# Output projection of a flow-matching backbone: 14 of 17 row tiles in pairs by seven products of quarters, with sums of the weights kept in DRAM

## The chip, the cores and the metric

The kernel runs on one core of one Trainium2 chip. The metric is device time in microseconds, from one launch to its end; of several executions the median counts. The profile comes from one further execution, whose own time is given beside its span.

## The reference, cut to what matters

One layer, no depth loop, two request groups: 128 context tokens and 2048 sample tokens, 2176 rows in all, 1024 channels. Input projection and three mixer branches stand ahead; what the change touches is the end:

```
gt = jax.nn.sigmoid(gates.reshape(B, T, N_BRANCH, D_MODEL))
merged = jnp.einsum('btnd,btnd->btd', gt, pb)
return jnp.einsum('btd,de->bte', merged, w_out), s_f, s_b
...
h = h + gate[:, None, :] * out
y_sample = rmsnorm(h, final_g)
```

So each of 17 tiles of 128 rows of `merged` is multiplied by the 1024 x 1024 matrix `w_out`, times a gate for each channel, plus the row of x, then a final RMSNorm. All is float32; the kernel splits each float32 operand into a high and a low half of float16 and makes three products (high by high, high by low, low by high) of each.

## The kernel before, in words

**Stages.** After the mixers come three merge passes (`merge`, lines 1672 to 1721), one for each branch. A pass runs over eight blocks of 128 channels; in each block it goes over two halves of the tokens, and for each group of up to 512 tokens it makes a gate product (24 matmuls, ScalarE takes the sigmoid from PSUM, L1699) and a branch product (12 matmuls, VectorE multiplies from PSUM, L1708); GpSimd adds the result to the row of partial sums, which is read from DRAM and written back there (`mD`, L1687, L1709, L1716). The rows live in the tag `mrow` of the pool `big`, two buffers.

**The last merge** (L1812) takes the upper half of the tokens first (tiles 8 to 16), then tiles 0 to 7. In each block it also loads one eighth of `w_out` and splits it (`out_w`, L1759, by `load_w`: a square for the scale on ScalarE, a scale by a one-column matmul and three small VectorE operations L264 to L266, a high half L311, a low half L312). In the last block, when the upper half is written, `ahead_out` (L1792) prepares the first five tiles in the order 16, 8, 9, 10, 11, while the last half's products still run. `out_prep` (L1765) loads a tile of the merged rows (SyncE, L1767), squares it (ScalarE, L1777), makes the scale, the high half (ScalarE, L1779), the low half (VectorE, L1780) and a row of eight scales (L1782).

**The output projection** (L1823 to 1863) takes the 17 tiles one by one. A tile is two halves of 512 columns, 24 matmuls each into one PSUM bank (`gemm_N`, L331): 48. VectorE multiplies each bank by the scaled gate (L1841), GpSimd adds the row of x (L1842); the gate itself is scaled for each tile by GpSimd (`scale_gate`, L1802). Then the row's square (ScalarE, L1860), a power on GpSimd (L251), the scaling of the row (VectorE, L1862) and the store. Tile i + 5 is prepared after tile i. The last tile has column groups of 512, 384 and 128 and its own end.

**What sets the order.** The kernel is written on a framework with pools of tiles. Each tag of a pool has a fixed number of buffers; a new tile takes a buffer in the order in which the text asks for it, and waits for the last reader of the tile before it. A pool that is opened where others were closed (`op`, L1816, after `big` and `bwp` are closed at L1813) takes their memory. The order of the instructions on each engine, and of the DMA issues on each queue, is fixed when the program is built: a planner takes, by its own estimate of the time, the instruction that is ready and comes first in the text; `tc.high_priority()` moves some forward. SyncE's loads and stores share one queue (SP), GpSimd's DMAs another.

The tag `wst` of the pool `wp`, two buffers of 128 x 1024, holds weights on their way in, and tiles of merged rows at the hand-over. `xh` and `xl` are the high and low halves of the normalised input, read by every gate product.

Of the kernel before, what the change touches and what calls it, by code (L numbers as in the profile page):

```python
# [20 lines left out]
P = 128  # L21
D = 1024
KT = 8
# [165 lines left out]
def hybrid_flow_kernel(ctx: ExitStack, tc: tile.TileContext, x_prompt, x_sample, state_delta, c, c_ctx, w_ada,  # L189
# [50 lines left out]
    def mm(out, l, r, start=True, stop=True):  # L240
        newest[0] = PE.matmul(out, l, r, start=start, stop=stop)  # L241
# [98 lines left out]
    def xrows(t0, n):  # L340
        return xs_[t0:t0 + n, :] if t0 < NS else xp_[t0 - NS:t0 - NS + n, :]
# [1415 lines left out]
    winv = sb(orp, [P, KT], "winv8")  # L1757

    def out_w(i):  # L1759
        w = load_w(w_outb[i], KT, hi=whi[:, :, i * P:(i + 1) * P], lo=wlo[:, :, i * P:(i + 1) * P])  # L1760
        V.tensor_mul(winv[:, i:i + 1], w.inv, sx)

    turn = []

    def out_prep(t, pl, tag, hl=None):  # L1765
        mt = sb(pl, [P, KT, P], tag, bufs=2)
        SY.dma_start(mt, mD[:, :, t * P:(t + 1) * P].rearrange("k p t -> p k t"))  # L1767
        if hl is None:
            mh = sb(orp, [P, KT, P], "mh", F16, bufs=3)
            ml = sb(orp, [P, KT, P], "ml", F16, bufs=3)  # L1770
        else:
            mh = sb(wp, [P, KT, P], "whi", F16, bufs=4)
            ml = sb(wp, [P, KT, P], "wlo", F16, bufs=4)
        ss = sb(orp, [P, 1], "mss", bufs=2)
        with tc.high_priority():
            with tc.issue_after(turn[0].ins) if len(turn) > 2 else ExitStack():
                A.activation(ml, mt, AF.Square, accum_out=ss)  # L1777
            s, inv = scales(ss, orp, "msc")
            turn.append(A.activation(mh, mt, AF.Copy, scale=s))  # L1779
            V.scalar_tensor_tensor(ml, mt, s, mh, ALU.mult, ALU.subtract)  # L1780
        inv8 = sb(orp, [P, KT], "inv8", bufs=6)
        V.tensor_scalar(inv8, winv, inv, None, ALU.mult)  # L1782
        return mh, ml, inv8

    pre, gp = [], []

    def half_gate(i):
        t = sb(ep, [P, 512], "st", bufs=3)
        SY.dma_start(t, gateD[1:2, i * 512:(i + 1) * 512].to_broadcast([P, 512]))
        gp.append(t)  # L1790

    def ahead_out(h0):  # L1792
        if h0:
            for i, t in enumerate(order[:5]):
                pre.append(out_prep(t, *((wp, "wst") if i % 3 else (big, "mrow")), None if i < 3 else wp))
            for i in range(2):
                half_gate(i)
                scale_gate(gp[i], gp[i], pre[0][2][:, 4 * i:4 * i + 4])
# [6 lines left out]
    order = [16] + list(range(8, 16)) + list(range(8))  # L1805
    def tail(db):
        out_w(db)
        if db == KT - 1:
            for _ in gates:
                pass  # L1810
# [5 lines left out]
    op = pool(ctx, "op", 2)  # L1816
    gb = sb(op, [P, D], "gb", bufs=1)
    SY.dma_start(gb, gateD[0:1, :].to_broadcast([P, D]))
    fg = sb(op, [P, D], "fg", bufs=1)
    SY.dma_start(fg, final_g[None, :].to_broadcast([P, D]))  # L1820

    part = sb(op, [P, 3], "part", bufs=1)
    for i_, t in enumerate(order):  # L1823
        mh, ml, inv8 = pre[i_]
        end = i_ == 16
        xr = sb(op, [P, D], "xr")
        SY.dma_start(xr, xrows(t * P, P))
        hh = sb(op, [P, D], "hh")
        ss2 = sb(op, [P, 1], "hss")
        if i_:  # L1830
            gt = sb(op, [P, D], "gt")
            scale_gate(gt, gb, inv8)
        if end:
            hf = sb(op, [P, D], "gt")
        for i, (c0, c1) in enumerate([(0, 512), (512, 896), (896, D)] if end else [(0, 512), (512, D)]):
# [3 lines left out]
            dst, gc = (hh[:, cs], gt[:, cs]) if i_ else (gp[i], gp[i])  # L1839
# [10 lines left out]
        if i_ < 12:  # L1850
            pre.append(out_prep(order[i_ + 5], op, "mt"))
# [40 lines left out]
```

## Time and profile before

| what | value |
|---|---|
| runs shown | 2181.92, 2181.95, 2177.65 us |
| median | 2181.92 us |
| profiled execution, its own time | 2174.15 us |
| its span, first to last instruction | 2172.3 us |
| granted TensorE clock, mean | 0.995 |
| TensorE busy | 2102.9 us of the span |
| VectorE, ScalarE, GpSimd busy | 1314.2, 1037.8, 704.2 us |
| HBM read and written | 241.48 and 127.62 MB |
| last merge and output projection | about 1724 us to the end |

How to read it: the page names engines PE (TensorE), PEld (its weight loads), DVE (VectorE), ACT (ScalarE), POOL (GpSimd), SP (SyncE); a small q behind a name is that engine's instruction queue. A row of a group gives line, engine, operation, output<-inputs, shapes and count, then busy time and mean ns of one, then the idle time of the engine ahead of them and what ended it. A row of a time line gives start and duration in us, and in brackets the idle time ahead. A row of the windows gives, for a stretch, the busy time of PE, PEld, DVE, ACT and POOL (with the number of instructions), the granted clock, the share of the DMA engines and the GB/s. Columns named `x` behind a count merge that many instructions. Products are matmuls of L241, whatever stage they belong to.

### The profile page before, as it was taken

The page shows a single profiled execution, that of the slowest core. Times are in us where ns is not written, and L with a number is a line of the kernel's source. Part 1 is how long each engine was busy: PE and PEld are TensorE (multiplying, and loading weights), DVE is VectorE, ACT ScalarE, POOL GpSimd, SP SyncE. Part 2 cuts the span into 40 slices and gives each one's busy share as a digit, 9 for nine tenths or more (in the row PEclk, how much of TensorE's full clock was granted, in tenths as well). Part 3 has the DMA queues.
Part 4 walks back from the last instruction along what each step waited for, and adds up shares of the span by engine and source line. Part 5 has one row for each costly group of instructions (what it writes and reads, how often), then busy time and mean ns, then how long its engine had stood idle before and what let it go on. Part 6 is the DMA issues. An engine that isn't in the chain of part 4 may idle for free. (4 is left out here: it accounts for less than half of the span.)

```text
span 2172.3 us, 42588 instructions
## 1 busy us (share of the span) xinstructions
PE 2102.9 (97%) x16249; PEld 1204.3 (55%) x16249; DVE 1314.2 (60%) x3049; ACT 1037.8 (48%) x2388; POOL 704.2 (32%) x869
## 2 busy tenths in 40 slices
PE   8999999999899999999899999899999999999998
PEld 4455444465455677787455556556555544444444
DVE  6657754389779798466655556765563544233454
ACT  5554744466556664455544446655553422222332
POOL 0321332233434422444222223354532222212543
PEclk9999999999999999999999999999999999999999
DMA  9525632276776743444755556776664533334542
GB/s 353 218 72 201 250 119 83 93 234 218 235 235 218 227 141 91 138 142 119 234 163 160 164 168 188 239 216 198 195 199 139 177 129 122 114 102 132 170 149 103
DMA packets 228748, 371.90 MB, mean 171 GB/s; under 512 B 38952, under 2 KB 125504, under 8 KB 226240
## 3 DMA queue, kind: packets, MB, share of 16 engines
q1 hardware_dynamic: 176032, 274.20, 40.3%
q0 software_dynamic: 12688, 51.27, 6.5%
q10 hardware_dynamic: 39824, 43.72, 6.0%
q8 instruction: 127, 2.08, 0.4%
q14 instruction: 77, 0.63, 0.1%
HBM read 241.48 MB, written 127.62 MB: 170 GB/s over the span
## 5 line engine op out<-in xcount | busy, mean ns | idle before, releaser
L241 PE MATMUL b<-xh,whi 128*128 128x512 f16 (+1 forms) x1920 | 649.7, 347 | 2.8 <-DVE sg L1436 2.5
L241 PE MATMUL b<-xl,whi 128*128 128x512 f16 (+1 forms) x1920 | 650.0, 347 | 0.0
L241 PE MATMUL b<-xh,wlo 128*128 128x512 f16 (+1 forms) x1920 | 649.0, 347 | 0.0
L241 PEld LDWEIGHTS <-whi 128*128 128x128 f16 x3904 | 355.7, 98 | 327.9 <-issue 8.6
L241 PEld LDWEIGHTS <-wlo 128*128 128x128 f16 x1952 | 191.0, 98 | 176.9 <-issue 1.4
L241 PE MATMUL b<-big,bhi 128*128 128x512 f16 (+1 forms) x960 | 250.8, 347 | 4.2 <-ACT big L1669 2.6
L1709 POOL TENSOR_TENSOR mrow<-mrow,sg 128x512 f32<-128x512 f32 (+1 forms) x80 | 93.4, 1169 | 283.2 <-DVE sg L1708 173.0
L241 PE MATMUL b<-big,blo 128*128 128x512 f16 (+1 forms) x480 | 162.9, 347 | 0.2 <-DVE blo L312 0.2
L1699 ACT ACTIVATE sg<-b,winv 128x512 f32<-128x512 f32 (+1 forms) x120 | 74.1, 618 | 132.6 <-PE b L241 132.1
L241 PEld LDWEIGHTS <-xh 128*128 128x128 f16 x1496 | 118.3, 99 | 30.0 <-issue 1.8
L1708 DVE SCALAR_TENSOR_TENSOR sg<-b,binv,sg 128x512 f32<-128x512 f32 (+1 forms) x80 | 53.4, 668 | 129.0 <-PE b L241 120.8
L241 PEld LDWEIGHTS <-bhi 128*128 128x128 f16 x960 | 86.4, 98 | 79.8 <-issue 4.4
L936 POOL TENSOR_TENSOR cy<-cy,raw 128x545 f32<-128x545 f32 (+1 forms) x48 | 64.4, 1366 | 180.6 <-ACT raw L935 180.6
L255 DVE CAST wscb<-wss 128x1 bf16<-128x1 f32 x89 | 13.7, 154 | 138.2 <-ACT wlo L299 57.6
L241 PE MATMUL b<-whi,xh 128*128 128x128 f16 x544 | 94.5, 221 | 1.8 <-DVE yT L1622 1.0
L1170 POOL COPY T<-ES 32x256 f16<-32x256 f16 x68 | 29.2, 430 | 201.2 <-DMA ES<-ei 178.2
L241 PE MATMUL b<-wlo,xh 128*128 128x128 f16 x544 | 94.4, 221 | 0.0
L241 PE MATMUL b<-whi,xl 128*128 128x128 f16 x544 | 94.4, 221 | 0.0
L241 PE MATMUL b<-wohi,mh 128*128 128x512 f16 (+2 forms) x248 | 91.9, 372 | 0.2 <-ACT mh L1779 0.2
L241 PE MATMUL b<-wohi,ml 128*128 128x512 f16 (+2 forms) x248 | 91.7, 372 | 0.3 <-DVE ml L1780 0.3
L241 PE MATMUL b<-wolo,mh 128*128 128x512 f16 (+2 forms) x248 | 91.9, 372 | 0.0
L312 DVE SCALAR_TENSOR_TENSOR wlo<-wst,wsc,whi 128x1024 f16<-128x1024 f32 x52 | 71.2, 1370 | 33.1 <-ACT whi L311 32.9
(481 smaller groups left out, 4241.3 us busy)
## 6 DMA issues: line engine op xcount, KB each, us to landing
wst<-in_w_blk_dram SPq DMA_DIRECT2D x58, 512.0 KB, 5.7
qkv<-cy POOLq DMA_DIRECT2D x12, 1089.0 KB, 5.3
st<-br SPq DMA_DIRECT2D x48, 256.0 KB, 3.8
mrow<-mrg SPq DMA_DIRECT2D x18, 512.0 KB, 3.8
mrow<-mrg SPq DMA_DIRECT2D x16, 576.0 KB, 4.4
mrg<-mrow POOLq DMA_DIRECT2D x16, 576.0 KB, 3.9
dc<-dec SPq DMA_DIRECT2D x17, 512.0 KB, 4.4
kq<-qkv SPq DMA_DIRECT2D x34, 256.0 KB, 4.9
```

What stands on the lines that cost most here:

```text
L241: newest[0] = PE.matmul(out, l, r, start=start, stop=stop)
L255: V.tensor_copy(sb16, ss)
L312: w.low = V.scalar_tensor_tensor(w.lo, st, s, w.hi, ALU.mult, ALU.subtract)
L936: G.tensor_tensor(y[:, c0:c1], y[:, c0:c1], raw[:, 1 + c0:1 + c1], ALU.mult)
L1170: G.tensor_copy(T16[rows(a0, b), :, :, b], ES[0:32, :, 2 * a0 + b, :, wT])
L1699: A.activation(sg, ps, AF.Sigmoid, scale=gw.inv)
L1708: V.scalar_tensor_tensor(sg, ps, binv[:, 1:2], sg, ALU.mult, ALU.mult)
L1709: G.tensor_tensor(mr, mr, sg, ALU.add)
```

## The change

Tiles 8 to 15 and 0 to 5 are taken in seven pairs; tiles 16 (first), 6 and 7 (last) stay single. A pair is a matrix of 256 rows by 1024 channels, cut into four quarters a11 to a22 (128 rows by 512 channels); `w_out` is cut into quarters b11 to b22 of 512 by 512. The pair is made from seven products of quarters, by Strassen's scheme in Winograd's form, in place of eight: four sums of quarters of the rows (s1 to s4), four of the weights, and sums of the results. Each product is 12 matmuls of 512 columns, and two of the three PSUM banks of a pair are added into twice.

What is added and moved, part by part:

- `out_w` runs in every second block of the last merge and takes two blocks of `w_out`, which share a scale; GpSimd makes the four differences of the weights, ScalarE and VectorE split them, GpSimd's queue stores them in DRAM (`tD`). After the merge SyncE loads them into the room of `xl` (four loads of 1 MB).
- the x rows and the result rows stand in the room of `xh`, in two sets of two rows each.
- ahead of the stage, tile 16 is prepared (`single`, in `wst`) and pair 8 (`pair_of`: its two tiles of rows in `wst`, its sums in two buffers of `mrow`). Pair 10 is prepared after tile 16, in the pool `op`; from then on pair i + 2 after pair i. Two buffers of operands alternate between pools `orp` and `op`.
- `pair_of`: two sums on GpSimd (s1, s3), two on VectorE (s2, s4), two squares, one scale for the pair, four high halves on ScalarE and four low halves on VectorE (three of 1024 columns, one of 512).
- `two_tiles`: the products; one copy from PSUM on ScalarE, five additions from PSUM on VectorE, one multiplication from PSUM on VectorE; GpSimd multiplies by the gate and adds x (seven operations of 512 columns a pair). The gate is scaled for a pair by ScalarE (`gates_of`), after the weights' scale has been multiplied in once.

The diff, cut to its core (the body of `one_tile` is the old loop's):

```
+    tD = dram("tw", [4, P, 4, 2 * 4 * P], F16)
+    def operands(pl):
+        return sb(pl, [P, 2, 7, 4, P], "pa", F16, bufs=1)
+    desk = operands(orp).rearrange("p l n k c -> p (l n k c)")
...
+    def out_w(j):
+        for st, i in zip(sts, (j, j + 4)):
+            SY.dma_start(st, w_outb[i].rearrange("p (k c) -> p k c", c=P))
...
+        for i in range(2):
+            A.activation(whi[:, :, cols_[i]], sts[i], AF.Copy, scale=s)
+            V.scalar_tensor_tensor(wlo[:, :, cols_[i]], sts[i], s, whi[:, :, cols_[i]], ALU.mult, ALU.subtract)
...
+        for q, out, x, y in ((0, t1, b12, b11), (1, t2, b22, t1), (2, t1, b22, b12), (3, t2, b21, t2)):
+            G.tensor_tensor(out, x, y, ALU.subtract)
+            slot = slots[:, (4 * j + q) % 3]
+            halves(slot[:, 0], slot[:, 1], out, s)
+            G.dma_start(tD[q, :, j, :], slot.rearrange("p l k c -> p (l k c)"))
...
+    def halves(hi, lo, src, s):
+        A.activation(hi, src, AF.Copy, scale=s)
+        V.scalar_tensor_tensor(lo, src, s, hi, ALU.mult, ALU.subtract)
...
+    def pair_of(t, pa, pl, tag, pls, tags):
+        m1, m2 = [sb(pl, [P, KT, P], tag, bufs=2) for _ in range(2)]
+        sums = [sb(pls, [P, 1024 if tags == "S" else 1152], tags, bufs=2)[:, 0:1024].rearrange("p (n k c) -> p n k c", n=2, k=4) for _ in range(2)]
+        merged(m2, t + 1)
+        merged(m1, t)
...
+        G.tensor_tensor(s1, a21, a22, ALU.add)
+        A.activation(flat(3, 5, 1), m2, AF.Square, accum_out=ss[:, 1:2])
+        A.activation(flat(5, 7, 1), m1, AF.Square, accum_out=ss[:, 0:1])
+        V.tensor_tensor(s2, s1, a11, ALU.subtract)
+        G.tensor_tensor(s3, a11, a21, ALU.subtract)
+        V.tensor_tensor(s4, a12, s2, ALU.subtract)
+        s = scaled(ss, inv)
+        for n0, n1, src in ((1, 3, m1), (3, 5, sums[0] ...), (5, 7, sums[1] ...), (0, 1, a22)):
+            halves(flat(n0, n1, 0), flat(n0, n1, 1), src, s)
...
     def ahead_out(h0):
         if h0:
-            for i, t in enumerate(order[:5]):
-                pre.append(out_prep(t, *((wp, "wst") if i % 3 else (big, "mrow")), None if i < 3 else wp))
+            pre.append(single(16, [m16[:, 0], m16[:, 1]], wp, "wst"))
...
+            pre.append(pair_of(8, operands(orp), wp, "wst", big, "mrow"))
...
+    tw = xl.rearrange("p k t -> p (k t)")[:, 0:16 * D].rearrange("p (q j l k c) -> p q j l k c", q=4, j=4, l=2, k=4)
+    for q in (1, 2, 0, 3):
+        SY.dma_start(tw[:, q].rearrange("p j l k c -> p j (l k c)"), tD[q])
...
+    def two_tiles(t, prepared):
...
+        def gated(j, cs):
+            G.tensor_tensor(hh[j][:, cs], hh[j][:, cs], gt[:, cs], ALU.mult)
+            G.tensor_tensor(hh[j][:, cs], hh[j][:, cs], xr[j][:, cs], ALU.add)
...
+        product(a, pa, 1, quarter(0, 0), True)
+            A.copy(p1, a)
+        product(Y, pa, 4, summed(1), True)
+        total(u2, Y, p1)
+        product(a, pa, 2, quarter(4, 0), False)
+            V.tensor_tensor(hh[0][:, left], a, gt[:, left], ALU.mult)
+        G.tensor_tensor(hh[0][:, left], hh[0][:, left], xr[0][:, left], ALU.add)
+        product(Y, pa, 5, summed(2), False)
+        total(u3, Y, p1)
+        product(X, pa, 3, summed(0), True)
+        total(hh[1][:, right], X, u3)
+        gated(1, right)
+        product(Y, pa, 0, summed(3), False)
+        total(hh[1][:, left], Y, p1)
+        gated(1, left)
+        product(X, pa, 6, quarter(4, 512), False)
+        total(hh[0][:, right], X, u2)
+        gated(0, right)
+        for j in (1, 0):
+            rows_done(t + j, hh[j], xr[j])
...
+            ready[firsts[i]] = pair_of(firsts[i], operands(op if i % 2 else orp), op, "mt", op, "S")
...
+    SY.dma_start(gb, gateD[0:1, :].to_broadcast([P, D]))
+    scale_gate(gb, gb, winv)
+    SY.dma_start(fg, final_g[None, :].to_broadcast([P, D]))
+    one_tile(16, pre[0])
+    prepare(1)
+    for i, t in enumerate(firsts):
+        two_tiles(t, ready[t])
+        prepare(i + 2)
+    one_tile(6, ready[6])
+    one_tile(7, ready[7], True)
```

More of the change, by code (lines that the diff above doesn't have):

```diff
@@ L238, in hybrid_flow_kernel, with mm @@
     newest = [None]
-    def mm(out, l, r, start=True, stop=True):
-        newest[0] = PE.matmul(out, l, r, start=start, stop=stop)
+    def mm(out, l, r, start=True, stop=True, reopened=False):
+        newest[0] = PE.matmul(out, l, r, start=start, stop=stop, skip_group_check=reopened)
     def mm3(out, l, r, start=True, stop=True):
```

177 lines of the change are left out of this document (116 added, 61 removed).

## The prediction, on record before the result

> **What bounds the kernel now.** I read the busy table first, then the chain that ended last, then the groups of instructions of the last 330 us, then the time lines of single engines at the hand-over from the last merge to the output projection.
>
> ```profile
> PE 2102.9 (97%) x16249; PEld 1204.3 (55%) x16249; DVE 1314.2 (60%) x3049; ACT 1037.8 (48%) x2388; POOL 704.2 (32%) x869
> 1660.97 310.97 PE b L241 x1729
> ...
> 1989.05 175.92 PE b L241 x851
> 2165.32 0.72 DVE hh L1842
> ```
>
> TensorE bounds it: the whole stage to be changed is one unbroken piece of products, 175.92 us, with a tail of some 7 us behind it (span 2172.3). 17 tiles of 48 products of 512 columns are 816, so one costs 175.92/816 = 0.2156 us, the few one-column products for the scales included, and a tile 10.35 us. That is a pitch, not a duration:
>
> ```profile
> L241 PE MATMUL b<-wohi,mh 128*128 128x512 f16 x232 | 87.9, 379 | 0.2 <-ACT mh L1779 0.2
> 2050.00:2100.00 50.00, 50.00 (x238) 22.70 (x236) 26.35 (x49) 17.19 (x25) 24.46 (x20) 1.00 0.44 146
> ```
>
> A record shows 379 ns, but 238 products start in 50 us, 0.210 each, at full granted clock. The Trainium skill (Perfetto Trace Analysis, "Engine Utilization") says that matmul busy time misleads because matmuls are pipelined; by the records the products taken out here would be worth 31.8 us, by the pitch 18.1, and the trace agrees with the pitch.
>
> The rest of the stage runs beside it. Its groups:
>
> ```profile
> L1842 POOL TENSOR_TENSOR hh<-hh,xr 128x512 f32<-128x512 f32 x30 | 37.9, 1266 | 71.7 <-DVE hh L1841 40.0 <-issue 24.7 <-DVE msc L266 4.4
> L1802 POOL TENSOR_TENSOR gt<-gb,inv 128x1024 f32<-128x1024 f32 x16 | 31.3, 1956 | 9.6 <-DMA gb<-gate 9.6
> L1841 DVE TENSOR_TENSOR hh<-b,gt 128x512 f32<-128x512 f32 x31 | 21.3, 687 | 24.0 <-PE b L241 21.5 <-POOL gt L1802 2.4
> L1862 DVE SCALAR_TENSOR_TENSOR hh<-hh,hss,fg 128x1024 f32<-128x1024 f32 x16 | 20.5, 1284 | 14.1 <-POOL hss L251 14.1
> L1780 DVE SCALAR_TENSOR_TENSOR ml<-mt,msc,mh 128x1024 f16<-128x1024 f32 x12 | 16.5, 1373 | 0.5
> L1779 ACT ACTIVATE mh<-mt,msc 128x1024 f16<-128x1024 f32 x12 | 13.8, 1148 | 38.4 <-DVE msc L265 38.4
> L1777 ACT ACTIVATE ml<-mt 128x1024 f16<-128x1024 f32 x12 | 12.7, 1057 | 38.6 <-PE b L241 29.2 <-DMA mt<-mrg 9.3
> L251 POOL TENSOR_TENSOR hss<-hss,mhalf 128x1 f32<-128x1 f32 x16 | 8.8, 550 | 1.8 <-DVE hss L250 1.8
> L264 DVE TENSOR_SCALAR msc<-b 128x1 int32<-128x1 int32 x17 | 2.5, 150 | 1.5 <-PE b L241 1.4
> L312 DVE SCALAR_TENSOR_TENSOR blo<-wst,wsc,bhi 128x512 f16<-128x512 f32 x4 | 3.0, 752 | 0.0
> ```
>
> **VectorE and GpSimd get in each other's way.** The time lines show it:
>
> ```profile
> 1985.31 0.23 DVE L1782 TENSOR_SCALAR inv<-winv,msc 128x8 f32<-128x8 f32 x1
> 2057.41 1.08 DVE L1782 TENSOR_SCALAR inv<-winv,msc 128x8 f32<-128x8 f32 x1
> 2057.20 1.27 POOL L1842 TENSOR_TENSOR hh<-hh,xr 128x512 f32<-128x512 f32 x1 [2.06 <-issue]
> 2022.48 2.50 POOL L1842 TENSOR_TENSOR hh<-hh,xr 128x512 f32<-128x512 f32 x2 [4.36 <-DVE msc L266]
> 2023.70 2.36 DVE L1780 SCALAR_TENSOR_TENSOR ml<-mt,msc,mh 128x1024 f16<-128x1024 f32 x1
> 2024.94 2.88 POOL L1802 TENSOR_TENSOR gt<-gb,inv 128x1024 f32<-128x1024 f32 x1
> ```
>
> The same tiny L1782 takes 0.23 us alone and 1.08 beside a GpSimd add, ending with it (2058.49 and 2058.47). The L1780 that begins at 2023.70 takes 2.36: it gets through only after GpSimd's pair of adds ends at 2024.98, and the next GpSimd operation, an L1802 of 1.96 in the mean, waits for it and takes 2.88. So a GpSimd operation and a VectorE operation with two operands in SBUF do not overlap; one waits the other out. The Trainium skill (SBUF — State Buffer, "Who interferes with whom") calls it an exclusive lock on a shared pair of ports, and exempts VectorE operations with at most one SBUF input; the trace agrees, and its own waits give the prices.
>
> **The change, part by part.**
>
> *Products.* A pair now takes 7 x 12 = 84 products in place of 96: 7 x 12 x 0.2156 = **-18.1 us**. A pair takes 18.1 us of TensorE, where two tiles took 20.7.
>
> *Weights' sums in the last merge.* Four times, four GpSimd subtractions (1.27 each), four copies on ScalarE, four low halves on VectorE (0.75) and four stores on GpSimd's queue. They lie under products: the piece of 310.97 us is unbroken, and an evacuation may be 7.7 us late there before a PSUM bank is missed (three banks; a gate product group of 24 and a branch group of 12 stand between). I take 0. Without this cover one chain of 4 x (1.27 + 0.75 + 0.75) = 11 us would miss by 3, 13 us in all; four fewer scales save under 1.
>
> *The hand-over.* Let T be 1987.7, when tile 16's low half and its first products begin.
>
> ```profile
> 1976.45 0.38 SPq L1767 DMA_DIRECT2D mrow<-mrg  x1
> 1976.92 2.27 SPq L1767 DMA_DIRECT2D wst<-mrg  x2
> 1989.02 0.33 SPq L1687 DMA_DIRECT2D mrow<-mrg  x1
> ...
> 2001.27 0.33 SPq L1818 DMA_DIRECT2D gb<-gate  x1
> ...
> 2002.61 0.43 SPq L1767 DMA_DIRECT2D mt<-mrg  x1
> 1980.83 1.06 ACT L1777 ACTIVATE ml<-mrow 128x1024 f16<-128x1024 f32 x1 [2.94 <-DMA mrow<-mrg]
> 1984.91 1.06 ACT L1777 ACTIVATE ml<-wst 128x1024 f16<-128x1024 f32 x1 [1.13 <-DMA wst<-mrg]
> 2011.36 1.06 ACT L1777 ACTIVATE ml<-mt 128x1024 f16<-128x1024 f32 x1 [7.32 <-DMA mt<-mrg]
> 1987.71 1.28 DVE L1780 SCALAR_TENSOR_TENSOR ml<-mrow,msc,mh 128x1024 f16<-128x1024 f32 x1 [2.17 <-ACT mh L1779]
> 1999.86 1.28 DVE L1780 SCALAR_TENSOR_TENSOR wlo<-mrow,msc,whi 128x1024 f16<-128x1024 f32 x1 [0.29 <-ACT whi L1779]
> 1992.84 2.50 POOL L1709 TENSOR_TENSOR mrow<-mrow,sg 128x512 f32<-128x512 f32 x2 [5.12 <-DMA mrow<-mrg]
> mrg<-mrow POOLq DMA_DIRECT2D x1, 512.0 KB, 3.0
> ```
>
> Buffers go out in the order of the text: the last merge row, ready long before, is loaded at 1989.02, when tile 16's low half (1987.71 + 1.28) frees its buffer. And `op`, the stage's pool, opens as a whole: gb goes out at 2001.27, when the last prepared row in the old pool is done (1999.86 + 1.28). Five tiles, 51 us of products, covered that. Now only tile 16 and pair 8 are ahead, 28.5 us.
>
> First wait: tile 16 and pair 8 need three `wst` buffers, and there are two. Tile 9's block goes out when tile 16's low half is done, T + 1.3; behind it on SP stands the last merge row. Ahead of it stand the four loads of weights' sums (4.19 MB) and some of the x rows, released when the last gate products end, 12 products before T, so at T - 2.6. Early in the kernel the DMAs moved 412 GB/s (last column):
>
> ```profile
> 10.00:20.00 10.00, 9.54 (x52) 4.46 (x50) 5.48 (x10) 6.79 (x13) 1.92 (x1) 1.00 1.03 412
> 38.00:42.00 4.00, 2.08 (x5) 0.69 (x5) 3.96 (x10) 2.94 (x6) 0.00 (x0) 0.74 1.09 448
> 42.00:46.00 4.00, 4.00 (x17) 1.74 (x16) 3.93 (x7) 4.00 (x7) 0.00 (x0) 0.83 0.93 386
> ```
>
> At that rate the sums take 10.2 us and two x rows 2.5. Of the three tile blocks issued from 1976.45 on, the first was used 4.4 us after its issue and the third 4.1 after that: 2.05 each, 2.3 fixed. Landing: T - 2.6 + 2.3 + 10.2 + 2.5 + 2.05 = T + 14.4. Then the square (1.06), the scale (four steps of 0.15 like L264), the copy (1.15) and the low half (1.28), 4.2 with a hand-over: pair 8 starts at T + 18.6, not T + 10.4. **+8.2** (0 if the block goes out ahead of the sums; 9.5 behind all three x rows).
>
> Second wait: the last merge row needs the buffer of pair 8's first sums, free one low half later, T + 19.9; then 3.8 from load to add, adds of 2.5, the store's landing 3.0: `op` opens at T + 29.2. Behind that wait on SP stand gb, fg and pair 10's two blocks. Four such loads, gb to mt, were issued from 2001.27 and the last was used at 2011.36, 10.1 later: T + 39.3, prepared at T + 43.5. Pair 8's products end at T + 36.7: **+6.8**. The wait of TensorE near 40 us (above, 2.08 busy of 4) goes with granted clocks of 0.74 and 0.83 over 4 us each, 1.7 us lost: **+1.7** once, as the first wait's loss is covered by the second.
>
> *The steady pairs.* On GpSimd a pair has nine operations of 512 columns (two sums, seven behind the products) and two powers: 9 x 1.27 + 2 x 0.55 = 12.5 us. VectorE has, with two SBUF operands, low halves of 3 x 1.28 + 0.75, two sums (unknown, between L1841's 0.69 and L312's 0.75; I take 0.7) and two row scalings of 1.28: 8.6. As these exclude each other, a pair needs 21.1 us against TensorE's 18.1; before, two tiles needed 4 x 1.27 + 2 x 1.96 + 2 x 0.55 + 4 x 1.28 = 15.2 of 20.7. Six pairs lack 3.0 each, 18 us. The two single tiles at the end need 2 x 1.27 + 0.55 + 2 x 1.28 = 5.7 of their 10.35 each and take up some 6 of the arrears: **+12**. The ends: 0, if the rows of a pair may trail in the second set of row buffers to the stage's end; +23, with 0.1 us lost at each of 18 hand-overs of a pair. ScalarE's some 10 us a pair (four squares, four and a half copies, an evacuation) and the five other evacuations (0.69, one SBUF operand, each due within 12 products, 2.6 us) fit beside it.
>
> *Sum*: -18.1 + 8.2 + 6.8 + 1.7 + 12 = **+10.6 us**. The profiled execution took 2174.15, 7.8 under the median of the runs shown; laid on that median of 2181.92 the forecast is 2192.5, 0.5% slower.
>
> **The rivals.**
>
> *The products decide* (faster). If tile 9's block goes out ahead of the sums and `op` opens tile by tile, the waits shrink to some 3 us, and if the rows' work on GpSimd trails, TensorE keeps its 18.1: -18 + 3 + 1, **2168**. For it: two sets of row buffers, the gate scaling taken over by ScalarE, and only six pairs in which to fall behind. Against: 21.1 us in 18.1, six times running. It decides where a pair's exclusive work is under 18.1 us.
>
> *The waits without the port*: 16.7 - 18.1 = -1.4, **2181**. For it: L1862 keeps 1284 ns in the mean, so the order can keep the two engines apart. Against: the sum of the durations.
>
> *The port without the waits*: -18.1 + 3 + 18, no arrears being taken up in a wait: +3, **2185**. For it: the orders of SP are a plan's, and the block may go first. Against: in the rows above, SP's order follows readiness, and the sums are ready 3.9 us sooner.
>
> *A pile-up*: each engine's order is fixed at build; a low half that waits for GpSimd holds the evacuation behind it past its 2.6 us, and every pair loses 6 and not 3: **2210**.
>
> **How the numbers follow.** Chances: the forecast (waits and port) 0.55; products decide 0.11; waits alone 0.11; port alone 0.11; pile-up 0.12. A measurement of this kernel can tell about 0.2%, 4.4 us, from no change. Slower: 0.52 of the forecast, 0.03 of the waits alone, 0.05 of the port alone, the pile-up's 0.12: 0.72. Same: 0.03 + 0.07 + 0.06 = 0.16. Faster: 0.11 and 0.01 of the waits alone. The range leaves out the fast rival and the pile-up's far half, 0.17: from half of both waits and half of the port (-18 + 8 + 6, 2178) to all waits and the port with hand-overs, and some more (-18 + 18 + 23, 2205, to 2209).
>
> **What would show it.** Right: pair 8's products beginning 6 us or more after tile 16's, behind its low half; TensorE idle again before pair 10, with gb issued around T + 29; later pairs starting every 20 to 23 us, the low halves on VectorE well above 1.28 us in the mean, and GpSimd busy for over half of the stage. Wrong: an unbroken chain of TensorE, pairs every 18 us; or a gap in the last merge, which would belong to the weights' sums.

## The result, and the profile after

The changed kernel takes 2213.74 us in the median of four runs (2211.27 to 2221.23), the kernel before 2179.78 beside it (2175.69 to 2181.95): ratio 1.0164, 95% interval 1.0134 to 1.0194. It is slower, as forecast, but by 34 us and not by 10.6, and the time lies above the range.

The first view of the changed kernel's page is the table of busy times:

```profile
PE 2103.7 (95%) x16154; PEld 1198.4 (54%) x16154; DVE 1359.8 (61%) x3049; ACT 1071.8 (48%) x2434; POOL 768.3 (35%) x921
```

TensorE has 95 products fewer than before and is busy 0.8 us longer: a product must have become slower somewhere. The windows over the last merge and over the output stage say where, first two of the kernel before, then two of the changed kernel (its profiled execution took 2214.17, its span is 2212.4; columns are the stretch, its length, busy time of PE, PEld, DVE, ACT and POOL, granted clock, share of the DMA engines, GB/s):

```profile
1718.91:1987.73 268.82, 268.58 (x1481) 130.04 (x1478) 96.45 (x249) 74.16 (x120) 55.79 (x58) 1.00 0.36 116
1987.73:2164.96 177.23, 176.94 (x855) 81.45 (x855) 88.98 (x166) 53.20 (x79) 83.71 (x69) 1.00 0.45 149
```

```profile
1723.95:2000.49 276.54, 270.94 (x1475) 130.43 (x1473) 105.57 (x239) 79.91 (x129) 84.34 (x89) 0.99 0.38 129
2000.49:2204.96 204.47, 172.81 (x766) 75.12 (x764) 128.27 (x173) 77.68 (x110) 113.29 (x88) 0.93 0.42 144
```

The last merge takes 276.5 us (268.8 before: +7.7), the stage from tile 16's first product to the end of the last product 204.5 (177.2 before: +27.2), at a granted clock of 0.93. The tail behind it is 7.4 in both. TensorE's order ahead of the last merge is the same in both kernels; that part ends at 1718.9 in the one profile (not at about 1724, as the table of the kernel before has it) and at 1723.9 in the other, and in twelve more profiles below between 1718 and 1735. So I compare these two stages, and leave the rest to the ratios. The two stages lose 34.9 us together; the medians differ by 34.0.

What TensorE waits for from 1700 us on (total, times, longest; one row of 0.6 us is left out):

```profile
PE b L241 <- ACT pa L1810: 17.2, 7, 3.9
PE b L241 <- DVE mss L1804: 5.7, 2, 4.3
PE b L241 <- DVE st L1972: 5.7, 2, 4.5
PE b L241 <- DVE sg L1708: 4.0, 2, 2.8
PE b L241 <- POOL xh L1968: 2.3, 1, 2.3
PE b L241 <- ACT sg L1699: 1.7, 2, 1.2
```

Before, there were two waits, of 0.3 and 0.2. The two rows with `sg` are the last merge. `mss`, `st` and `xh` are the start of the stage, but for one wait of 1.5 and one of 1.2. Of the first row 14.8 us are four waits of the steady pairs, 3.4 to 4.0 each.

**The start.** Its landmarks came nearly where the forecast had put them (T is 2000.49, tile 16's first product). SyncE's queue and two rows of TensorE:

```profile
1996.56 1.62 SPq L1879 DMA_DIRECT2D xl<-tw  x2
2001.99 0.37 SPq L1795 DMA_DIRECT2D wst<-mrg  x1
2020.31 0.32 SPq L1687 DMA_DIRECT2D mrow<-mrg  x1
2030.17 0.32 SPq L2007 DMA_DIRECT2D gb<-gate  x1
...
```

```profile
2038.16 1.44 PE L241 MATMUL b<-xl,pa 128*128 128x512 f16 x3 [4.50 <-DVE st L1972]
...
2048.46 0.38 PE L241 MATMUL b<-wohi,pa 128*128 128x512 f16 x1 [2.26 <-POOL xh L1968]
```

Tile 9's block goes out at T + 1.5 (forecast T + 1.3) and pair 8 begins at 2017.82, T + 17.3 (18.6); the last merge row is asked for at T + 19.8 (19.9) and gb at T + 29.7 (29.2). Pair 10 begins at T + 48.0 (43.5). Not forecast is the row between: TensorE stands for 4.5 us inside pair 8, because its evacuation waits on VectorE behind tile 16's row scaling, and that for fg:

```profile
2036.05 1.45 DVE L1902 SCALAR_TENSOR_TENSOR xh<-xh,hss,fg 128x1024 f32<-128x1024 f32 x1 [4.36 <-DMA fg<-in_final_g_dram]
2037.43 0.68 DVE L1972 TENSOR_TENSOR st<-b,sg 128x512 f32<-128x512 f32 x1
```

**The steady pairs.** Four pairs are 340 products, scales included: 94.64 us, 23.7 a pair. Below that row, one turn in windows of 4 us:

```profile
2064.32:2158.96 94.64, 78.39 (x340) 33.85 (x341) 66.21 (x86) 39.38 (x57) 59.87 (x44) 0.95 0.40 131
2084.00:2088.00 4.00, 0.28 (x2) 0.00 (x0) 2.32 (x6) 0.97 (x1) 1.41 (x2) 1.00 0.79 281
2088.00:2092.00 4.00, 3.77 (x11) 1.43 (x12) 3.79 (x4) 3.91 (x5) 1.77 (x1) 0.57 0.47 154
2092.00:2096.00 4.00, 4.00 (x20) 1.83 (x19) 3.77 (x3) 0.00 (x0) 3.92 (x3) 1.00 0.21 63
...
2112.00:2116.00 4.00, 4.00 (x12) 1.44 (x13) 4.00 (x4) 3.59 (x4) 2.08 (x1) 0.58 0.50 154
```

Once in a pair TensorE stands for some four microseconds, and in the next four it starts 11 or 12 products in place of 20, at a granted clock of 0.57 or 0.58. So a pair is in the mean 18.3 us of products, 4.1 of waiting ((94.64 - 78.39) / 4) and 1.3 of slow products (78.39 / 4 - 18.3). Three slow stretches lie in these four pairs, at 1.7 us each (4 us at 0.57); the fourth begins where they end. The Trainium skill (TensorE: Matmul & The Clock Gate, "Part 1: The HAM clock gate (the “warmup” mystery)") says that an idle window of some 3.4 us halves TensorE's clock until it has been busy for about as long; the rows agree (waits of some 4 us, then 4 us at 0.57). In other places shorter waits were followed by a slow clock too (2.8 us in the last merge; see the last section).

Why does it stand? VectorE's time line ahead of 2112, and below it GpSimd's and ScalarE's:

```profile
2102.40 0.68 DVE L1972 TENSOR_TENSOR st<-b,sg 128x512 f32<-128x512 f32 x1
2104.31 2.28 DVE L1902 SCALAR_TENSOR_TENSOR xh<-xh,hss,fg 128x1024 f32<-128x1024 f32 x1 [1.23 <-POOL hss L251]
2106.51 0.15 DVE L1804 TENSOR_TENSOR mss<-mss 128x1 bf16<-128x1 f32 x1
2106.58 0.68 DVE L1981 TENSOR_TENSOR xh<-b,gt 128x512 f32<-128x512 f32 x1
2107.18 0.14 DVE L250 TENSOR_SCALAR hss<-hss 128x1 f32<-128x1 f32 x1
2109.14 1.28 DVE L1902 SCALAR_TENSOR_TENSOR xh<-xh,hss,fg 128x1024 f32<-128x1024 f32 x1 [1.82 <-POOL hss L251]
2110.34 0.15 DVE L264 TENSOR_SCALAR msc<-b 128x1 int32<-128x1 int32 x1
```

```profile
2102.50 1.27 POOL L1967 TENSOR_TENSOR xh<-xh,gt 128x512 f32<-128x512 f32 x1 [1.23 <-DVE hss L250]
...
2104.24 1.26 POOL L1968 TENSOR_TENSOR xh<-xh 128x512 f32<-128x512 f32 x1
...
2108.55 0.55 POOL L251 TENSOR_TENSOR hss<-hss,mhalf 128x1 f32<-128x1 f32 x1
```

```profile
2101.94 0.18 ACT L1837 ACTIVATION_READ_ACCUMULATOR pa<-mt 128x1 f32 x1
...
2110.71 1.15 ACT L1810 ACTIVATE pa<-mt,msc 128x1024 f16<-128x1024 f32 x1 [4.03 <-DVE msc L265]
```

The squares of the next pair are done at 2102.1. Their sum (L1804) is ready to go, but stands behind the first row scaling of the pair before (L1902), which waits for GpSimd's power and then takes 2.28 us beside a GpSimd addition; the scale (L264) stands behind the second scaling, which waits again, for 1.82. The copy that TensorE wants begins at 2110.71, 8.6 us behind the squares, of which the scale's own instructions need one.

**The last merge.** Three time lines around its longest wait (ScalarE, VectorE, TensorE):

```profile
1742.90 1.06 ACT L1777 ACTIVATE wolo<-pa 128x1024 f16<-128x1024 f32 x1 [1.85 <-DMA pa<-in_w_outb_dram]
```

```profile
1744.08 0.20 DVE L1779 TENSOR_TENSOR oss2b<-oss 128x1 bf16<-128x1 f32 x1 [2.93 <-ACT wolo L1777]
...
1744.76 0.74 DVE L1708 SCALAR_TENSOR_TENSOR sg<-b,binv,sg 128x512 f32<-128x512 f32 x1
```

```profile
1745.56 0.38 PE L241 MATMUL b<-xh,whi 128*128 128x512 f16 x1 [2.79 <-DVE sg L1708]
```

The second block of `w_out` lands late; its square holds ScalarE, the sum of squares VectorE, and the evacuation behind that sum is 2.8 us late for TensorE. Of the 7.7 us that the merge loses, 5.6 are waits (276.54 - 270.94, 0.2 before). The rest, some 2, is slower products: TensorE is busy for 270.9 us in place of 268.6, and behind this longest wait the granted clock is 0.64 over 4 us.

### The profile page after: what moved, and what is told of

It is laid out like the page before. It is cut to its first block, busy times and chain, and to the rows that moved or that the text cites. A ratio compares the mean times of both kernels' runs of the same rounds, so it can differ in the third digit from the quotient of the medians.

```text
span 2212.4 us, 42506 instructions
## 1 busy us (share of the span) xinstructions
PE 2103.7 (95%) x16154; PEld 1198.4 (54%) x16154; DVE 1359.8 (61%) x3049; ACT 1071.8 (48%) x2434; POOL 768.3 (35%) x921
## 5 line engine op out<-in xcount | busy, mean ns | idle before, releaser
L241 PEld LDWEIGHTS <-whi 128*128 128x128 f16 x3840 | 350.6, 98 | 327.4 <-issue 16.3
L241 PEld LDWEIGHTS <-pa 128*128 128x128 f16 x660 | 65.0, 102 | 116.2 <-ACT pa L1810 25.8
L1170 POOL COPY T<-ES 32x256 f16<-32x256 f16 x68 | 29.2, 430 | 199.3 <-DMA ES<-ei 166.2
L241 PE MATMUL b<-xl,pa 128*128 128x512 f16 x336 | 85.7, 411 | 6.2 <-DVE st L1972 5.7
L299 ACT ACTIVATE wlo<-wst 128x1024 f16<-128x1024 f32 x52 | 55.0, 1058 | 70.2 <-DMA wst<-in_w_blk_dram 65.2
```

What stands on the lines that cost most here:

```text
L241: newest[0] = PE.matmul(out, l, r, start=start, stop=stop, skip_group_check=reopened)
L299: w.squared = A.activation(w.lo, st, AF.Square, accum_out=ss)
L1170: G.tensor_copy(T16[rows(a0, b), :, :, b], ES[0:32, :, 2 * a0 + b, :, wT])
```

## The experiments

Theories: **A**, the port: operations of VectorE and GpSimd with two operands in SBUF add up (21.1 us a pair in the forecast). **B**, the order: on VectorE's fixed queue the next scale stands behind row scalings that wait for GpSimd. **C**, the start: buffers, or the transfers. **D**, the weights' sums in the last merge. The results in one table; merge and stage are of each kernel's profiled execution, the period is taken over 340 products (170, 255 or 364 where the order is uneven; in e9_inturn and e10_turn over the last two pairs between two like waits):

| kernel | last merge | output stage | period | time | ratio to before |
|---|---|---|---|---|---|
| before | 268.8 | 177.2 | 20.7 | | 1 |
| changed | 276.5 | 204.5 | 23.7 | 2213.7 | 1.0164 [1.0134, 1.0194] |
| e1_order | 275.6 | 194.0 | 21.0 | 2202.6 | 1.0101 [1.0076, 1.0126] |
| e2_nosum | 271.3 | 203.6 | 23.7 | 2211.5 | 1.0157 [1.0129, 1.0184] |
| e3_singles | 275.1 | 195.8 | 23.6 | 2208.0 | 1.0128 [1.0098, 1.0158] |
| e4_nogate | 275.9 | 187.0 | 19.4 | 2193.1 | 1.0073 [1.0048, 1.0097] |
| e5_all | 275.5 | 180.5 | 21.1 | 2193.4, one run | |
| e6_vector | 274.4 | 170.8 | 19.1 | 2183.8 | 1.0015 [0.9993, 1.0037] |
| e7_all_nogate | 276.6 | 168.4 | 19.2 | 2178.0, one run | |
| e8_split | 271.3 | 170.8 | 19.1 | 2177.5 | 0.9987 [0.9970, 1.0003] |
| e9_inturn | 270.0 | 186.2 | 22.2 | 2194.2 | 1.0059 [1.0041, 1.0077] |
| e10_turn | 276.8 | 200.4 | 21.8 | 2209.7 | 1.0126 [1.0107, 1.0145] |
| e11_rows | 270.9 | 171.5 | 19.5 | 2176.6 | 0.9988 [0.9972, 1.0004] |
| e12_loads | 273.7 | 202.8 | 23.6 | 2206.1, one run | |

The tail behind the last product is not in the table: it is 7.4 in both kernels, 6.6 to 8.1 in e1, e2, e4, e10 and e12, and 8.9 to 10.6 in the others.

**e1_order: only VectorE's order** (`made[0]` is the last instruction of the next pair's scale).

```
-        V.scalar_tensor_tensor(hh, hh, ss2, fg, ALU.mult, ALU.mult)
+        owed.append((t, hh, ss2))
...
         two_tiles(t, ready[t])
         prepare(i + 2)
+        pay()
...
+    def pay():
+        with tc.issue_after(made[0].ins):
+            for t, hh, ss2 in owed:
+                V.scalar_tensor_tensor(hh, hh, ss2, fg, ALU.mult, ALU.mult)
...
```

> The row scalings of a pair are put behind the scale of the next prepared pair on VectorE; nothing else differs. Theory B (order: the scale of the next pair waits in VectorE's queue behind the row scalings, which wait for GpSimd): the wait of TensorE of 3.6 to 4.1 us ahead of each pair shrinks to 1 us or less, the pairs' period falls from 23.6 to some 21, five periods and the end: 2213.7 - 13 = about 2201. Theory A (port: VectorE's and GpSimd's work with two operands exclude each other, 21.1 us a pair and more): the same work stands in another order, the period stays over 23, the time within 4 us of 2213.7.

Measured: period 21.0, stage 194.0 (-10.5), time 2202.6. VectorE's time line now, at the same place in a pair:

```profile
2101.16 0.15 DVE L1804 TENSOR_TENSOR mss<-mss 128x1 bf16<-128x1 f32 x1
...
2101.89 0.14 DVE L264 TENSOR_SCALAR msc<-b 128x1 int32<-128x1 int32 x1
...
2102.38 3.20 DVE L1907 SCALAR_TENSOR_TENSOR xh<-xh,hss,fg 128x1024 f32<-128x1024 f32 x2
```

```profile
2061.71:2103.45 41.74, 37.28 (x171) 16.31 (x170) 32.07 (x43) 19.54 (x29) 29.93 (x22) 1.00 0.46 150
```

Sum and scale are 0.7 us apart, not 3.8, and the clock is 1.00 again. B is shown, at 2.7 us a pair. What is left, 21.0, is what A alone had priced (21.1). But the time lines do not show the shared resource full: the operations of GpSimd and those of VectorE that read no PSUM cover, overlaps counted once, 38.3 of these 41.7 us. That period and sum agree so closely does not prove A's size.

**e2_nosum: the last merge without the sums.**

```
-        for q, out, x, y in ((0, t1, b12, b11), (1, t2, b22, t1), (2, t1, b22, b12), (3, t2, b21, t2)):
-            G.tensor_tensor(out, x, y, ALU.subtract)
-            halves(slot[:, 0], slot[:, 1], out, s)
-            G.dma_start(tD[q, :, j, :], slot.rearrange("p l k c -> p (l k c)"))
+        for q in range(4):
+            G.dma_start(tD[q, :, j, :], (whi, wlo)[q // 2][:, :, cols_[q % 2]])
```

> The four differences of the weights and their halves are left out of the last merge (parts of the weights' own halves are stored in their place, with the same four stores), so the products with sums of weights have other factors. Theory D (the sums' work on GpSimd and VectorE holds evacuations back in the last merge): the last merge goes back from 276.5 us to some 269.5, the time falls by about 7 to 2207. If the 7.7 us are not the sums' (new order of the blocks, the pairing of weights' blocks, the clock): the merge stays at 276, the time at 2213.7 within 2 us.

Measured: the merge 271.3, so 5.2 of its 7.7 us hang on the sums; 2.5 remain. D holds for the larger part. The time, 2211.5, fell by 2 and not by 7; the runs of this kernel scatter over 7 us.

**e3_singles: tiles 16 and 8 single and first.**

```
+    pairs = [(9, 10), (11, 12), (13, 14), (15, 0), (1, 2), (3, 4), (5, 6)]
...
-            pre.append(pair_of(8, operands(orp), wp, "wst", big, "mrow"))
+            pre.append(single(8, halved(orp), wp, "wst"))
...
     one_tile(16, pre[0])
+    prepare(0)
+    one_tile(8, pre[1])
...
```

> The single tiles are 16 and 8 (first) and 7 (last); the pairs are 9 with 10 to 5 with 6, all prepared in the stage's own pool. No sums stand in the merge rows' buffers, and two weight buffers do for the tiles that are prepared ahead. Theory C (start-up: third weight buffer, and merge rows' buffers that hold the pool's opening back): the first pair starts where two single tiles end, T + 20.7, give or take 2, in place of losing 19.5 us by the second pair; with one single tile less at the end, whose loss of 7 stays: about 15 to 17 us less, 2197 to 2199. Rival: the start is bound by the transfers of 4 MB of weights' sums and of rows, whoever asks first: the first pair starts at T + 28 or later, gain under 8, 2206 or more.

Measured: stage -8.7, the first pair at T + 27.9 and not at T + 20.7; the rival's place, with a gain between the two. The rows of its DMA issues (KB each, median us to landing) and SyncE's queue (T is 2005.44):

```profile
xl<-tw SPq DMA_DIRECT2D x4, 1024.0 KB, 14.6
...
mrg<-mrow POOLq DMA_DIRECT2D x1, 512.0 KB, 8.7
```

```profile
2002.32 1.13 SPq L1883 DMA_DIRECT2D xl<-tw  x2
2017.99 0.32 SPq L2010 DMA_DIRECT2D gb<-gate  x1
```

No buffer holds the last merge row back now, but its store, issued at 2009.18, lands 8.7 us later in place of 3.0, behind the 4 MB of weights' sums, and the stage's pool opens with it.

**e4_nogate: less work on GpSimd.**

```
         def gated(j, cs):
-            G.tensor_tensor(hh[j][:, cs], hh[j][:, cs], gt[:, cs], ALU.mult)
             G.tensor_tensor(hh[j][:, cs], hh[j][:, cs], xr[j][:, cs], ALU.add)
```

> GpSimd's three multiplications by the gate of each pair are left out, so three quarters of a pair's rows lack the gate. Theory A: exclusive work falls by 3 x 1.27 = 3.8 us a pair, from 21.1 to 17.3, under TensorE's 18.1; the period falls by 3.8 or more to under 20 and the low halves fall back from 2.29 us towards 1.28; 2213.7 - 5 x 3.8 - 3 = about 2191. Theory B: GpSimd's power and with it the row scalings come earlier too, but they still stand ahead of the scale of the next pair; the period falls by 2 at most, 2203 or more, and the low halves beside sums and additions stay near 2 us.

Measured: period 19.4, time 2193.1, as A had it; the row scalings fall to 1292 ns in the mean (1661 in the changed kernel), but the low halves of the sums do not (1699 against 1784). So B and A are not two separate costs, as I read it: B's price is GpSimd's lateness, and with 3.8 us less on GpSimd most of it goes without a change of order.

**e5_all: e1 and e3, with the sums' loads behind the first pair's rows** (`asked[0]` is the last load of those rows).

```
-    for q in (1, 2, 0, 3):
-        SY.dma_start(tw[:, q].rearrange("p j l k c -> p j (l k c)"), tD[q])
...
     prepare(0)
+    with tc.issue_after(asked[0].ins):
+        for q in (1, 2, 0, 3):
+            SY.dma_start(tw[:, q].rearrange("p j l k c -> p j (l k c)"), tD[q])
```

> Row scalings behind the next scale, as in e1_order, and single tiles 16 and 8 first, as in e3_singles, and in addition the four loads of the weights' sums (4 MB) asked for behind the rows of the first pair, not ahead of the last merge row's store. From the profiles so far: the output stage took 204.5 us in the changed kernel; the order took 10.5 off, the single tiles 8.7, and the first pair still began 7.2 us late, behind the store and loads that the sums held up. If the transfers' order is that cause: the first pair at T + 21 to 23, stage 204.5 - 10.5 - 8.7 - 6 = about 179, time about 2188. If it is the amount of the transfers and not their order: the first pair at T + 27 or its second product waits as long, stage 185, time 2195. The period of the pairs stays at 21 in both.

Measured: the first pair at T + 22.0, stage 180.5, time 2193.4 and not 2188. The order of the transfers was the cause of the late start that e3 had left: the store of the last merge row lands in 3.0 again, and e1's order alone, which is in e5 too, does not bring the first pair forward (T + 18 in e1_order, T + 17.3 in the changed kernel).

**e6_vector: GpSimd's two-operand work on VectorE.**

```
-            G.tensor_tensor(hh[j][:, cs], hh[j][:, cs], gt[:, cs], ALU.mult)
+            V.tensor_tensor(hh[j][:, cs], hh[j][:, cs], gt[:, cs], ALU.mult)
...
-        G.tensor_tensor(s1, a21, a22, ALU.add)
+        V.tensor_tensor(s1, a21, a22, ALU.add)
```

and so for s3 and the weights' differences.

> e5_all, with GpSimd's operations of two operands moved to VectorE where they can be: both sums of rows (2 a pair), the gate's multiplication (3 a pair) and the weights' differences (4 in every second block of the last merge). Nothing is left out. Theory A (a sum of exclusive work): VectorE 3 x 1.28 + 0.75 + 2 x 1.28 + 7 x 0.7 = 12.1, GpSimd 4 x 1.27 + 2 x 0.55 = 6.2, together 18.3 us a pair: the period falls from 21.0 to 18.3 or 19, the stage to about 162, and with the last merge at some 272 the time is about 2213.7 - 25 - 16 - 4 = 2168, faster than before. Rival (the fixed order of one queue sets it, and VectorE, then busy for 17.3 of 18.1 us a pair, holds evacuations back): period 20.5 or more, 2185 or more.

Measured: period 19.1, stage 170.8, 6.5 under before; ratio 1.0015, no difference that can be told, since the last merge still takes 5.6 more than before and the tail 2.1 more. The window of four pairs:

```profile
2058.09:2134.64 76.55, 73.63 (x340) 32.83 (x340) 67.27 (x105) 39.27 (x57) 27.57 (x24) 1.00 0.50 163
```

VectorE is busy for 16.8 us of a pair and GpSimd for 6.9, and TensorE loses 0.7 ((76.55 - 73.63) / 4). A is right in direction and nearly in size (18.3 or 19 forecast). The time missed its forecast of 2168 by 16: the 16 us that I expected from the pairs came out as 10 in the stage, and the merge fell by 1 and not by 4.

**e7_all_nogate: e5 without the gate's multiplications** (the line of e4 taken out of e5).

> e5_all without GpSimd's three multiplications by the gate in each pair, which leaves the gate out of three quarters of a pair's rows. Exclusive work 17.3 us a pair, under TensorE's 18.1. Theory A with the order mended: the period falls from 21.0 to 18.1 to 18.5, the stage to about 161. If a wait of another kind is left: the period stays over 19 (19.35 with the multiplications left out and the order as it was).

Measured: period 19.2, stage 168.4: the second case, a wait of another kind. Exclusive work of 17.3 (18.3 in e6) does not bring the period below e6's 19.1, so there A's sum no longer sets it. What does is not shown; TensorE's waits are many and short (the longest from 1980 us on is 0.9).

**e8_split: e6 with the loads of `w_out`'s blocks put one block of the merge ahead of the work on them.**

```
     def tail(db):
-        if db % 2 == 0:
-            out_w(db // 2)
+        (out_w if db % 2 else out_load)(db // 2)
...
```

> e6_vector, with the two blocks of the output weights asked for one block of the last merge (some 33 us) before their squares, scale, halves and sums are made. In e6_vector the last merge still lost 5.6 us against before, 3.3 of it with a sigmoid of ScalarE standing behind squares that waited for their block's transfer. If the order of loads and squares is that cause: waits of TensorE in the last merge under 2 us, the merge at 269 to 271 in place of 274.4, the time 4 us less than e6_vector's, about 2180, ratio to before 0.998 to 1.001. If it is the amount of the work on ScalarE and VectorE: the merge stays at 274, the ratio at 1.0015.

Measured: the merge 271.3 (-3.1), the stage unchanged, ratio 0.9987 [0.9970, 1.0003]. But the loads did not get a block's lead. SyncE asks for the second two blocks just when the halves and differences of the first two are done (the last difference ends at 1777.39), and the first square still waits for its block, as it does for the third and fourth two. SyncE's queue and ScalarE:

```profile
1777.10 0.88 SPq L1775 DMA_DIRECT2D pa<-in_w_outb_dram  x2
```

```profile
1782.90 1.06 ACT L1781 ACTIVATE wolo<-pa 128x1024 f16<-128x1024 f32 x1 [3.50 <-DMA pa<-in_w_outb_dram]
```

From load to square are 5.8 us (4.5 in e6, 3.9 and 5.9 in the changed kernel). What the edit did move is the place: from the halves of the first two blocks on (1728.3 in e6, 4 us into the merge; 1769.9 here, 36 us into it) all this work comes one block of the merge later. So 3.1 of the 5.6 us that e6 lost in the merge go with the place of this work; that late blocks were the cause, as I had expected, is not shown.

**e12_loads: the same on the changed kernel alone.**

> The changed kernel, with the two blocks of the output weights asked for one block of the last merge before the work on them, and nothing else. Without the sums (e2_nosum) the merge still took 271.3 us, 2.5 over before. If those 2.5 are squares that wait for their blocks and hold a sigmoid back, and the 5.2 of the sums come from GpSimd and VectorE: the merge falls from 276.5 to about 274. If the loads are behind the sums' part too: the merge falls to 271 or less. If neither: it stays at 276.

Measured: 273.7, the value of the first case, but not for its reason: here too the second two blocks are asked for at 1764.81, 6 us ahead of their square. Of the 7.7 us, 2.8 go with the new place of the work alone, 5.2 without the sums, and 5.2 in e8 (the new place, and the sums on VectorE). These gains do not add up, because some 2 us are in each of them: in all three the longest wait is gone or short, the granted clock stays at 1.00, and TensorE is busy for 268.8 to 269.0 us in the merge in place of 270.9. The rest is waits: 5.6 in the changed kernel, 4.7 in e12, 2.6 in e8 and 2.3 without the sums.

**e9_inturn and e10_turn: TensorE's own order**, on e8 and on the changed kernel.

```
+        with tc.issue_after(last_[0].ins) if last_[0] else ExitStack():
             product(a, pa, 1, quarter(0, 0), True)
```

> e8_split, with the first product of a pair put behind the last product of the pair ahead on TensorE's queue (as planned, up to a dozen products of the next pair stand ahead of the last two dozen of the present one). If products that are ready and stand behind one that waits cost something: the waits of the pairs of 0.9 to 1.4 us go, the period falls from 19.1 to 18.5, the time by 3 to 4 us. If not: within 1 us of e8_split, or slower, since a product of the next pair no longer fills the place of one that waits for an evacuation.

> The changed kernel, with the first product of a pair put behind the last product of the pair ahead on TensorE's queue; nothing else differs. In the changed kernel three products of the next pair stand ahead of 24 of the present one, and the fourth or first of them waits 3.6 to 4.1 us for the next pair's scale. If that place on TensorE's own queue is part of the loss: the 24 products fill the wait, the pair's rows are done earlier, and with them the next scale; the period falls from 23.7 to 21 or 22, the time by 8 to 12 to about 2203. If VectorE's order alone decides: the wait moves behind the 24 products and stays as long, period 23 to 24, time within 3 us of 2213.7.

Measured: e9's stage is 186.2, 15.4 more than e8's: the second case (or slower), by more than I had thought. Its TensorE and VectorE, inside a pair:

```profile
2094.22 1.01 PE L241 MATMUL b<-xl,pa 128*128 128x512 f16 x2 [4.80 <-DVE st L1979]
```

```profile
2089.42 3.48 DVE L1815 SCALAR_TENSOR_TENSOR pa<-S,msc,pa 128x1024 f16<-128x1024 f32 x2
2092.82 0.74 DVE L1815 SCALAR_TENSOR_TENSOR pa<-mt,msc,pa 128x512 f16<-128x512 f32 x1
2093.49 0.68 DVE L1979 TENSOR_TENSOR st<-b,sg 128x512 f32<-128x512 f32 x1
```

Three low halves of the next pair stand ahead of an evacuation of this one, and one waits for a GpSimd addition. In e8 products of the next pair could fill such places. e10 gains 4.1 in the stage, less than the first case (8 to 12) and more than the second (3); its last two pairs take 21.8 each, as in the first case, but the earlier ones more: the wait put down to the copies falls from 17.2 us to 2.0, and others take its place, first of all these two:

```profile
PE b L241 <- DVE hss L250: 9.7, 3, 3.9
PE b L241 <- DVE st L1972: 6.9, 3, 5.0
```

TensorE's order is thus a small part of the loss at most, 4 of 27 us in the stage.

**e11_rows: e8 with the rows of every second pair in the merge's weight buffers.**

```
-operands(orp if i % 2 else op), op, "mt", op, "S")
+operands(orp if i % 2 else op), *((wp, "wst") if i % 2 else (op, "mt")), op, "S")
```

> e8_split, with the rows of every second prepared pair in the two weight buffers of the last merge in place of the stage's own, so that the second pair's rows are asked for ahead of the weights' sums and no longer wait for the first pair's low halves. In e8_split TensorE waits 3.2 us inside the first pair for the second pair's scale, and runs at a lower clock behind it. If those buffers are the cause: that wait goes, with what is lost in the clock some 4 to 5 us, the stage 166 in place of 170.8, the time about 2173, ratio to before 0.996 to 0.998. If VectorE, busy for nearly the whole pair, is the cause: the wait moves and the ratio stays at 0.9987.

Measured: the wait of 3.2 us for the second pair's scale is gone (in the first pair TensorE waits 1.5 us, 1.1 of it for a load of the weights' sums), but the stage is 171.5 and the ratio 0.9988. The wait moved, as its rival had it: the pairs take 19.5, and TensorE stands for 2.4 us for the last tile's low half, with a granted clock of 0.67 in the 4 us behind. Neither e8 nor e11 can be told from before for certain; both are better than the changed kernel by 1.7%.

## Why the prediction was wrong, point by point

The sign and the order of events held; the size did not. A stage without a wait would take 157.8 us (7 x 18.1 + 3 x 10.35). The changed kernel lost 19.5 up to the second pair (T + 48.0, not 28.5), 27.2 from there on, and 7.7 in the merge. With the -18.1 of the products that is 36.3, less the 1.3 us that the kernel before already loses in this stage (177.2 for 175.9): 35.0, against 34.9 measured. Of the 27.2 us, 25.2 fall in the pairs up to the wait that ends at 2158.96. Behind it TensorE does not wait again, as this row shows; 2.0 are lost there, nearly all to the slow clock behind that wait:

```profile
2158.96:2204.96 46.00, 46.00 (x230) 21.76 (x230) 27.73 (x41) 17.20 (x25) 24.64 (x21) 0.96 0.32 109
```

- *Products, -18.1*: right. The windows at full clock start 20 products in 4 us, and 340 products were busy for 73.6 us in e6, 18.4 a pair.
- *First wait, +8.2*: right but for 1.3 us, +6.9. The block was there 2.7 us sooner than worked out (T + 11.7), and its preparation took 5.6 and not 4.2.
- *Second wait, +6.8, and clock, +1.7*: the mechanism held to half a microsecond up to the opening of the pool, but the two together took 12.6 and not 8.5. I followed only who waits for the last transfer (pair 10), not what stands behind the others: tile 16's row scaling waited for fg on VectorE, and the evacuation behind it stopped pair 8. The clock fell after each long wait, not once. With single tiles first and another order of transfers (e5) the first pair starts only 1.3 us behind two unbroken tiles (T + 22.0 for 20.7).
- *The steady pairs, +12*: **the step that failed.** I added up exclusive work, 21.1 us a pair, and let it run without holes. The sum came close: with the order mended, e1 and e5 take 21.0 and 21.1, in part by luck, since the two engines leave 3.4 of e1's 41.7 us empty. But on each engine's queue the order is fixed, and there work of the old pair that waits for GpSimd stood ahead of the new pair's scale: +2.6 a pair, 1.3 of it through the clock, which I had taken to be paid once for the whole stage. Measured 27.2 in place of 12. That TensorE runs through the last pair and the last two tiles unbroken is as forecast, though the 6 us of arrears that I let the tiles take up were not worked out (2 x (10.35 - 5.7) is 9.3). The Trainium skill (TensorE: Matmul & The Clock Gate, "HAM oscillation — how this bites in real kernels") describes such a loop, whose wait crosses the idle window and which pays the slow start in every round; here 0.57 to 0.60 of the clock for 4 us, behind each of four waits.
- *The weights' sums, 0*: wrong, 7.7. The cover that I named, 7.7 us for an evacuation, holds between groups of 512 tokens; the longest wait came behind the group of 128, and with two engines in a row held by a block of `w_out` that was not there. I had put no wait on the new loads at all, though two blocks are now asked for at once. Without the sums 5.2 of it go, with the work one block later 2.8; the slow clock behind the longest wait, some 2 us, is in both.
- *The rivals*: the pile-up at 2210 had the size (6 a pair; 5.6 measured, 23.7 against 18.1) and the principle, one operation that waits for GpSimd and holds what stands behind it. The victim was another: the next scale behind row scalings. The form that it named, an evacuation behind a low half, is what e9 shows. That its total lies within 4 us of the measured time is in part luck: it counts 30 us for the pairs (27.2 measured) and nothing for the merge (7.7). *The products decide* did not come true even where its condition held: at 17.3 us of exclusive work the pairs took 19.2, not 18.1.

Not settled: the 1 us a pair and more that stays in e6 to e8 and e11 (in e6 0.3 of it are the products, 18.4 for 18.1, and 0.7 waits of 1 us and less), and whether late blocks or the place of the work cost the merge its waits.

## What to carry to other kernels

A sum of busy times on a shared resource is a rough lower bound; with queues whose order is fixed at build, look besides for each instruction that waits for the slowest engine, and ask what of the next round stands behind it. Where a stage waits once a round for 3.4 us or more, as here, price the slower clock behind each wait, not once. New work "under" a saturated engine is free only if its inputs have landed when its turn comes. To ask for them earlier helps only if a buffer is free for them by then: look in the trace whether the load really went out earlier.

## What the runs showed of the hardware

- Each of the four waits of TensorE of 3.4 to 4.0 us in the steady pairs of the changed kernel was followed by 4 us with 11 or 12 products of 20, at a granted clock of 0.57 to 0.60. In the profiles of the changed kernel and the twelve experiments all 30 waits of 3.4 us or more from 1715 us on were followed by a slow clock (0.50 to 0.67 over the next 4 us). Of the 23 waits of 2.2 to 3.2 us, 15 were (0.57 to 0.69) and 8 were not (1.00). The two rows, each of its own run, show the 4 us behind the same wait of the last merge, of 2.8 us in the changed kernel and of 3.1 in e3_singles:

```profile
1745.56:1749.56 4.00, 4.00 (x12) 1.49 (x12) 4.00 (x9) 0.00 (x0) 2.51 (x4) 0.64 0.00 0
```

```profile
1752.24:1756.24 4.00, 4.00 (x19) 1.85 (x19) 4.00 (x9) 0.00 (x0) 2.52 (x4) 1.00 0.00 0
```

- VectorE's row scaling took 1.28 us alone and 2.28 beside one GpSimd addition (2109.14 and 2104.31 above), while an addition with one operand in PSUM kept its 0.68 beside GpSimd's L1967 (2102.40 above).
- A 512 KB store landed in 3.0 us, and in 8.7 when four loads of 1 MB had been asked for ahead of it on another queue.
